# Reordered first loads, ten raw weight buffers and a pause of the background sums in a decoder layer on one core

## The chip, the core and the metric

The kernel runs on one core of one Trainium2 chip. The core has TensorE (PE in the profile, with its weight loads as PEld), VectorE (DVE), ScalarE (ACT), GpSimd (POOL) and SyncE (SP). Each takes its instructions in the order in which the compiler wrote them. Here SP and POOL also issue the DMAs. The metric is the device time of one execution in microseconds, lower is better; a kernel's time is the median of its runs.

## What is computed

One layer of a hybrid decoder for 256 tokens and a model width of 2048, all in float32. Cut to what matters here:

```python
mod = silu(c) @ w_ada + b_ada                 # 2048 -> 6 * 2048
shift1, scale1, gate1, shift2, scale2, gate2 = split(mod, 6)
h = rms_norm(x, norm1_gain) * (1 + scale1) + shift1
proj = h @ w_in                               # 2048 -> 13840 columns
qa = rms_norm(split_heads(q_sb, 6), sb_q_gain)          # stick-breaking attention, 6 heads
ka = rms_norm(split_heads(k_sb, 6), sb_k_gain)
o_sb = stick_breaking_attention(qa, ka, v_sb)
o_dil = dilated_mixture(rms_norm(q_dil), rms_norm(k_dil), v_dil)
o_gla = rms_norm(gated_linear_attention(q_gla, k_gla, v_gla, a)) * silu(r_gla)
g = sigmoid(gate_cols.reshape(256, 3, 2048))
y = g[:, 0] * (o_sb @ w_br_sb) + g[:, 1] * (o_dil @ w_br_dil) + g[:, 2] * (o_gla @ w_br_gla)
x = x + gate1 * (y @ w_out)
h = rms_norm(x, norm2_gain) * (1 + scale2) + shift2
gate, up = split(h @ w_ffn_in, 2)
x = x + gate2 * ((silu(gate) * up) @ w_ffn_out)
```

## The kernel before

**Three products for one.** Each float32 operand is split into a rounded high part and a low part (type fp32r). A product is then three matmuls: high by high, high by low and low by high (`mm3`, L180 to L182). A weight tile of two k blocks and 512 columns (128 x 1024 elements) is loaded by SP (L161) into a `raw` buffer, rounded on ScalarE into `whi` (L172), and subtracted on VectorE into `wlo` (L173). There are four buffers each of `whi` and `wlo` in the pool `wp`, and four of `raw`. `raw_tile` can add further raw buffers by name from other slots: `state["load_raws"]` for `load_weights`, `state["more_raws"]` for `load_pair`. It takes them in turn. For pairs of blocks the loads and splits have lines of their own (L228, L248, L234).

**A framework orders the work.** The kernel is written with named slots (`S("X1", ...)` takes the slot X1 when its last user is done) and priorities. The framework puts the instructions of each engine in a fixed order by priority and by its own model of time, and adds the waits. Loads, casts and splits of weights, and evictions of PSUM, stand in `prio()`, that is, 4000 places ahead of their place in the program. In `first_chunks` all of it has a still higher priority, and inside `in_order()` the program's order on PE, ScalarE and VectorE is kept.

**The start (`first_chunks`, from L632).** x comes transposed in four tiles `xT[j]` of 128 x 4 x 256, the small vectors (c, gains, biases) as `vec`, and the columns of the modulation's first chunk as `rows` from `ada_0`. `squares` (L543) squares a tile of x on ScalarE, adds its four parts in halves on VectorE (L550) and sums over partitions with a matmul by ones (L552). `root_of` (L554) makes the reciprocal root with a Newton step; between its exponential and the step it runs the work that is handed to it as `between`. The first chunk's scale and shift are made partly by PE (`on_pe`, `by_pe`, L730) and partly by VectorE (`on_dve`, L744), whose part PE sums at the end. `make_h` (L593 to L598) then writes the first chunk of the normed and modulated input h. `keep_warm(n)` (L710) issues n matmuls without use, in the numbers of `WARM`.

**The visits.** The input projection's first 13 blocks of 512 columns run while h grows chunk by chunk. `VISITS` lists which blocks run over which k; a block's partial sums lie in SBUF in between (evicted at L630, brought back at L618). `ada_chunks` meanwhile loads the columns of the modulation for the next chunk on SP's queue (L426) and reduces them on VectorE (`column_mac`, L433: one multiply-and-add with a sum per half column). In the visits `load_raws` is X1 and X2, so there are six raw buffers.

**The last visits.** `LAST` gives the k that are left of each block. Blocks 0 to 2 run, then `qk_norm` of the stick-breaking heads is called (squares on ScalarE L909, root L406 to L414, scaling on VectorE L917), then blocks 3 to 5. After that PE turns the heads (`qk_turn`, L929 and L930), and blocks 9 to 12 run with the steps of the stick-breaking attention between their products (`scores` from L949, with L952 and L953 on PE, L956 on VectorE, L959 to L961 on ScalarE). L1012 copies the product with `w_a` out of PSUM. Then come the GLA levels and blocks 6 to 8.

**Background sums.** From the last visits on, `background` makes the four other parts of the modulation (shift2, scale2, gate1, gate2), 32 half columns each, 128 in all. A step orders one 512 KB tile on GpSimd's queue (L426) into a ring of slots and runs the oldest waiting sum on VectorE (L433). At first the ring has the two slots AR0 and AR1. When a step is due is set by `tick`: a block ticks once per two k blocks with `state["rate"]`, a pair of blocks twice the rate per entry, and a step runs when the sum passes one. The rates stand in `RATE_*` and `RATES_*`. Before the output projection a loop runs steps until gate1 is there (L1469), at the third unit of the FFN `flush` runs all that is left.

**Later stages.** Two blocks for r; twelve gate blocks, of which three run singly first, six in three pairs (some entries of a pair use a fast product of seven matrices instead of eight) and three singly later, ahead of the last of the four blocks of branch products (`y_block`); then the output projection with `w_out`, the second norm, eleven FFN units, and the FFN's output.

Of the kernel before, what the change touches and what calls it, by code (L numbers as in the profile page):

```python
# [17 lines left out]
P = 128  # L18
# [14 lines left out]
SEG_SHIFT1, SEG_SCALE1, SEG_GATE1, SEG_SHIFT2, SEG_SCALE2, SEG_GATE2 = range(6)  # L33
RATE_IN, RATE_MID, RATE_GATES, RATE_PAIRS, RATE_Y, RATE_LAST = 0.7, 0.6, 0.6, (0.25, 0.2, 0.2), 0.55, 0.75

RATES_OP, RATES_FFN = (0.9, 0.7, 0.0), (0.75, 0.9, 0.7, 0.6)
LOOK = 3
DEFER = 4
AHEAD = 4000
WARM = (8, 2, 2, 2, 2, 3)  # L40
BADA = 58
RATE_FIRST = 0.7
BLOCKS_X, BLOCKS_Y, BLOCKS_Z = (1, 2, 3, 4), (5, 6, 7, 8), (9, 10, 11, 12, 0)
# [43 lines left out]
def trunk(ctx: ExitStack, tc: tile.TileContext, I, out):  # L87
# [454 lines left out]

    def squares(j, tag, a, b, sums):  # L543

        sq = S(tag, [P, 4, T]) if a == 0 else state["squares"]
        state["squares"] = sq
        nc.scalar.activation(sq[:, a:b], xT[j][:, a:b], AF.Square)
        n = (b - a) // 2
        while n:
            nc.vector.tensor_tensor(sq[:, a : a + n], sq[:, a : a + n], sq[:, a + n : a + 2 * n], op=ALU.add)  # L550
            n //= 2
        nc.tensor.matmul(sums, ones, sq[:, a, :], start=(j, a) == (0, 0), stop=(j, b) == (3, 4))  # L552

    def root_of(sums, between):  # L554


        act = nc.scalar.activation
        v, y, z, r = (x for x in S("X0", [P, 4, T]).rearrange("p a t -> a p t"))
        first = xT[0][:, 0, :]
        act(y, sums, AF.Ln, bias=eps_c[:, 0:1], scale=1.0 / D)  # L560
        nc.vector.tensor_scalar(v, sums, 1.0 / D, EPS, op0=ALU.mult, op1=ALU.add)
        act(y, y, AF.Exp, scale=-0.5)
        act(z, y, AF.Square)
        between()
        nc.vector.tensor_tensor(first, first, y, op=ALU.mult)
        nc.vector.tensor_mul(z, z, v)
        nc.vector.tensor_scalar(z, z, -0.5, 1.5, op0=ALU.mult, op1=ALU.add)
        nc.vector.tensor_tensor(first, first, z, op=ALU.mult)
        nc.vector.tensor_mul(r, y, z)
        return r  # L570
# [61 lines left out]
    def first_chunks():  # L632
# [56 lines left out]

        x_in(0, 0, 4)  # L690
        nc.sync.dma_start(vec, I["k_vec"])
        x_in(1, 0, 4)
        x_in(2, 0, 4)
        mods_in(0, 0, 4)
        x_in(3, 0, 2)
        x_in(3, 2, 4)
        mods_in(1, 0, 4)
        mods_in(2, 0, 4)
        mods_in(3, 0, 2)
        mods_in(3, 2, 4)  # L700
        load_two(0, 1, True)
# [10 lines left out]
        with in_order():  # L712
# [32 lines left out]

            squares(0, "X1", 0, 4, sums)
            keep_warm(WARM[2])
            squares(1, "X2", 0, 4, sums)
            keep_warm(WARM[3])
            squares(2, "AR0", 0, 4, sums)  # L750
            on_pe(0, 1)
            on_dve(2, 3)
            for a in (0, 2):
                squares(3, "AR1", a, a + 2, sums)
            r = state["root"] = root_of(sums, lambda: on_dve(6, 7))
            on_pe(4, 5)
            keep_warm(WARM[4])
            on_pe(8, 9)
# [12 lines left out]
            nc.vector.tensor_tensor(sh, mods[1], vec[:, o : o + 1], op=ALU.add)  # L771
            keep_warm(WARM[5])
            make_h(0, True)
# [85 lines left out]
    while steps < 4:  # L859
        next(chunks)  # L860
        steps += 1
    state["load_raws"] = ("X1", "X2")
    for n, (b, k0, k1, until) in enumerate(visits):
# [395 lines left out]
    gate2_v = columns_of("gate2")  # L1259
    bg.append(background())  # L1260
    state["rate"] = RATE_FIRST
    for b in range(0, 3):
        proj_block(*LAST[b], b)
    qk_norm(sb_parts)
    for b in range(3, 5):
# [508 lines left out]
```

## Time and profile before

| | us |
|---|---|
| median of 3 runs | 1602.7 (1599.18 to 1602.97) |
| profiled execution, device time | 1598.08 |
| its span, first to last instruction | 1596.3 |
| busy: PE, PEld | 1558.0, 1280.4 |
| busy: VectorE, ScalarE, GpSimd | 1373.4, 916.7, 71.8 |
| mean granted TensorE clock | 0.993 |
| moved by DMA | 399.20 MB, mean 250 GB/s |

The profile is of one execution. Busy time is the time in which an engine had an instruction running; matmuls overlap, and their ends are modelled, so PE counts as busy also where it isn't at its peak. The granted clock is the share of full speed that the chip gave TensorE. A row of the waits names the waiting engine, tile and line, then what released it, then the total in us, the number of times and the longest. Where an instruction waits for several things, the last one is named.

### The profile page before, as it was taken

What the parts mean: (1) busy time and instruction counts of PE and PEld (TensorE: products, weight loads), DVE (VectorE), ACT (ScalarE), POOL (GpSimd) and SP (SyncE); (2) the same over time, 40 slices, a digit from 0 to 9 for tenths busy, and PEclk for the clock granted to TensorE, in tenths of its full rate; (3) what the DMA queues carried; (4) which work ended last, traced back from release to release, by engine and by line L of the source; (5) the groups of instructions that cost most, each with busy time, mean ns of one, the idle gap of its engine ahead of it and who ended that gap; (6) DMA issues with size and microseconds to landing.
All of it is one profiled execution on the core that took longest, in us unless ns stands there. A gap on an engine that the chain in (4) does not pass through costs nothing.

```text
span 1596.3 us, 20113 instructions
## 1 busy us (share of the span) xinstructions
PE 1558.0 (98%) x7072; PEld 1280.4 (80%) x7072; DVE 1373.4 (86%) x1841; ACT 916.7 (57%) x1293; POOL 71.8 (5%) x139
## 2 busy tenths in 40 slices
PE   8999999899999999999999999999999999999998
PEld 7777777788787888888777888888888888888887
DVE  7888876879788989987988987999999999789886
ACT  6777676675755555344434745655655655455553
POOL 0000001100010000101210000000000000000000
PEclk9999999999999999999999999999999999999999
DMA  9999988766777776979989676666556566656664
GB/s 337 390 353 321 346 272 291 240 193 206 252 270 243 251 237 214 324 265 346 381 313 327 241 219 194 206 211 201 194 186 214 185 206 218 205 185 191 230 205 139
DMA packets 113924, 399.20 MB, mean 250 GB/s; under 512 B 12544, under 2 KB 13440, under 8 KB 113824
## 3 DMA queue, kind: packets, MB, share of 16 engines
q1 hardware_dynamic: 94816, 328.72, 60.6%
q0 software_dynamic: 19008, 69.21, 12.8%
q8 instruction: 55, 0.90, 0.2%
q14 instruction: 45, 0.37, 0.1%
HBM read 393.69 MB, written 4.19 MB: 249 GB/s over the span
## 4 chain that ended last, share of the span: by engine, by line
PE 50%; issue 27%; DMA 3%; POOL 3%; DVE 3%; ACT 1%; SPq 0%; POOLq 0%; DVEq 0%; ACTq 0%
PE acc L182 10%; PE acc L181 10%; PE acc L180 10%; PE misc L180 6%; PE misc L182 6%; PE misc L181 6%; DMA raw<-w_out 2%; POOL AR L426 2%; DVE wlo L173 1%; PE misc L1082 1%; POOL KC L426 1%; DMA KD<-ada_t 1%; POOL KD L426 1%; DMA AR<-ada_t 0%; DMA T<-k_lvl 0%
## 5 line engine op out<-in xcount | busy, mean ns | idle before, releaser
L181 PE MATMUL acc<-wlo,H 128*128 128x512 f32 (+1 forms) x856 | 336.3, 393 | 6.2 <-DVE wlo L173 3.9
L172 ACT CAST whi<-raw 128x1024 fp32r<-128x1024 f32 x220 | 225.9, 1034 | 200.2 <-PE acc L182 114.9
L180 PE MATMUL acc<-whi,H 128*128 128x512 f32 (+1 forms) x856 | 334.9, 395 | 5.8 <-ACT whi L172 5.8
L182 PE MATMUL acc<-whi,H 128*128 128x512 f32 (+1 forms) x856 | 335.4, 392 | 0.1
L173 DVE TENSOR_TENSOR wlo<-raw,whi 128x1024 fp32r<-128x1024 f32 x220 | 261.2, 1197 | 76.5 <-ACT whi L172 76.0
L181 PEld LDWEIGHTS acc<-wlo,H 128*128 128x128 f32 x856 | 161.9, 189 | 44.1 <-DVE wlo L173 8.8
L180 PEld LDWEIGHTS acc<-whi,H 128*128 128x128 f32 x856 | 161.6, 189 | 39.7 <-ACT whi L172 7.1
L182 PEld LDWEIGHTS acc<-whi,H 128*128 128x128 f32 x856 | 161.7, 189 | 33.5 <-DVE H L1515 0.5
L248 ACT CAST whi<-raw 128x1024 fp32r<-128x1024 f32 (+1 forms) x133 | 128.0, 977 | 75.3 <-PE acc L182 28.5
L234 DVE TENSOR_TENSOR wlo<-raw,whi 128x1024 fp32r<-128x1024 f32 (+1 forms) x133 | 147.9, 1127 | 16.4 <-ACT whi L248 15.2
L181 PE MATMUL misc<-wlo,H 128*128 128x512 f32 x285 | 111.4, 391 | 0.1
L182 PE MATMUL misc<-whi,H 128*128 128x512 f32 x285 | 110.5, 388 | 0.0
L180 PE MATMUL misc<-whi,H 128*128 128x512 f32 x285 | 108.6, 388 | 0.0
L182 PE MATMUL acc<-whi,A 128*128 128x512 f32 x221 | 86.1, 389 | 0.0
L181 PE MATMUL acc<-wlo,A 128*128 128x512 f32 x210 | 82.2, 391 | 3.6 <-DVE wlo L173 3.6
L180 PE MATMUL acc<-whi,A 128*128 128x512 f32 x210 | 82.1, 391 | 1.4 <-ACT whi L172 1.4
L173 DVE TENSOR_TENSOR wlo<-X,whi 128x1024 fp32r<-128x1024 f32 (+1 forms) x44 | 48.0, 1099 | 22.2 <-ACT whi L172 22.2
L181 PEld LDWEIGHTS misc<-wlo,H 128*128 128x128 f32 x285 | 53.5, 188 | 13.6 <-DVE wlo L173 2.9
L180 PEld LDWEIGHTS misc<-whi,H 128*128 128x128 f32 x285 | 53.5, 188 | 11.1
L182 PEld LDWEIGHTS misc<-whi,H 128*128 128x128 f32 x285 | 53.5, 188 | 10.8
L433 DVE CUSTOM_DVE_ANT_0 AR<-AR,ada,vec 128x1024 f32<-128x1024 f32 x36 | 46.0, 1278 | 13.9 <-DMA AR<-ada_t 13.9
L234 DVE TENSOR_TENSOR A<-raw,A 128x1024 fp32r<-128x1024 f32 (+2 forms) x58 | 54.3, 944 | 1.7 <-ACT A L248 0.9
(724 smaller groups left out, 3278.4 us busy)
## 6 DMA issues: line engine op xcount, KB each, us to landing
raw<-w_in SPq DMA_DIRECT2D x158, 512.0 KB, 5.1
raw<-w_ffn_in SPq DMA_DIRECT2D x137, 512.0 KB, 4.6
raw<-w_ffn_out SPq DMA_DIRECT2D x74, 512.0 KB, 4.3
AR<-ada_t POOLq DMA_DIRECT2D x70, 512.0 KB, 6.0
X<-w_in SPq DMA_DIRECT2D x39, 512.0 KB, 5.1
raw<-w_out SPq DMA_DIRECT2D x32, 512.0 KB, 7.0
OS<-ada_t SPq DMA_DIRECT2D x29, 512.0 KB, 7.3
KC<-ada_t POOLq DMA_DIRECT2D x22, 512.0 KB, 7.1
```

Of the source, the lines that this page charges most:

```text
L172: state["cast"] = nc.scalar.copy(hi[:, :n, :], raw[:, :n, :])
L173: state["split"] = nc.vector.tensor_tensor(lo[:, :n, :], raw[:, :n, :], hi[:, :n, :].bitcast(F32), op=ALU.subtract)
L180: nc.tensor.matmul(ps, lh, rh, start=start, stop=False, skip_group_check=seeded)
L181: nc.tensor.matmul(ps, lh, rl, start=False, stop=False, skip_group_check=seeded)
L182: state["mm"] = nc.tensor.matmul(ps, ll, rh, start=False, stop=stop, skip_group_check=seeded)
L234: done = nc.vector.tensor_tensor(dst, x, y, op=ALU.subtract)
L248: nc.scalar.copy(hi[:, :n, :], src)
L426: return queue.dma_start(raw, I["ada_t"][o : o + P, half * HALF : (half + 1) * HALF])
L433: return nc.vector.tensor_tensor_reduce(out=raw, in0=raw, in1=cB[:, half * HALF : (half + 1) * HALF], scale=1.0, scalar=part if half else ...
L1082: nc.tensor.matmul(ps[:n, t * N_GLA + h, :].rearrange("p (s l) -> p s l", l=L), at(f, h, t)[:, :n], odd(at(f, h, t)), start=True, stop=True,)
```

## The change

It has five parts. In the start, `vec` is loaded first, then the four tiles of x whole, then all tiles of `ada_0`; `squares` takes whole tiles with one addition on VectorE and two matmuls, and for the last tile VectorE squares one half; `root_of` has nothing in between any more, and the sums of chunks 6 and 7 follow it. The warming matmuls are dealt out anew: 23 instead of 19. In the visits `load_raws` gets four more slots, AR0, AR1, KC and KD, which makes ten raw buffers; ahead of the last visits it goes back to X1 and X2. The rate of the background is 0.0 in blocks 3 and 4, from `qk_norm` on. And eight rates have other numbers. The background's tiles stay on GpSimd's queue.

```diff
-RATE_IN, RATE_MID, RATE_GATES, RATE_PAIRS, RATE_Y, RATE_LAST = 0.7, 0.6, 0.6, (0.25, 0.2, 0.2), 0.55, 0.75
-RATES_OP, RATES_FFN = (0.9, 0.7, 0.0), (0.75, 0.9, 0.7, 0.6)
+RATE_IN, RATE_MID, RATE_GATES, RATE_PAIRS, RATE_Y, RATE_LAST = 0.8, 0.6, 0.65, (0.42, 0.25, 0.25), 0.55, 0.75
+RATES_OP, RATES_FFN = (0.9, 0.7, 0.0), (0.6, 0.75, 0.6, 0.5)
-WARM = (8, 2, 2, 2, 2, 3)
+WARM = (8, 2, 2, 2, 1, 2, 2, 4)
-RATE_FIRST = 0.7
+RATE_FIRST = 0.8
...
-    def squares(j, tag, a, b, sums):
-        sq = S(tag, [P, 4, T]) if a == 0 else state["squares"]
-        state["squares"] = sq
-        nc.scalar.activation(sq[:, a:b], xT[j][:, a:b], AF.Square)
-        n = (b - a) // 2
-        while n:
-            nc.vector.tensor_tensor(sq[:, a : a + n], sq[:, a : a + n], sq[:, a + n : a + 2 * n], op=ALU.add)
-            n //= 2
-        nc.tensor.matmul(sums, ones, sq[:, a, :], start=(j, a) == (0, 0), stop=(j, b) == (3, 4))
-    def root_of(sums, between):
+    def squares(j, tag, sums):
+        sq = S(tag, [P, 4, T])
+        if j < 3:
+            nc.scalar.activation(sq, xT[j], AF.Square)
+        else:
+            nc.scalar.activation(sq[:, :2], xT[j][:, :2], AF.Square)
+            nc.vector.tensor_tensor(sq[:, 2:], xT[j][:, 2:], xT[j][:, 2:], op=ALU.mult)
+        nc.vector.tensor_tensor(sq[:, :2], sq[:, :2], sq[:, 2:], op=ALU.add)
+        for n in range(2):
+            nc.tensor.matmul(sums, ones, sq[:, n, :], start=(j, n) == (0, 0), stop=(j, n) == (3, 1))
+    def root_of(sums):
...
-        between()
...
-        x_in(0, 0, 4)
         nc.sync.dma_start(vec, I["k_vec"])
-        x_in(1, 0, 4)
-        x_in(2, 0, 4)
-        mods_in(0, 0, 4)
-        x_in(3, 0, 2)
-        x_in(3, 2, 4)
-        mods_in(1, 0, 4)
-        mods_in(2, 0, 4)
-        mods_in(3, 0, 2)
-        mods_in(3, 2, 4)
+        for j in range(4):
+            nc.sync.dma_start(xT[j], I["x_t"][:, 4 * j : 4 * j + 4, :])
+        for j, a, b in ((0, 0, 4), (1, 0, 4), (2, 0, 4), (3, 0, 2), (3, 2, 4)):
+            nc.sync.dma_start(rows[j][:, a:b], I["ada_0"][:, 4 * j + a : 4 * j + b, :])
...
-            squares(2, "AR0", 0, 4, sums)
+            squares(2, "AR0", sums)
+            keep_warm(WARM[4])
+            squares(3, "AR1", sums)
+            on_dve(2, 3)
             on_pe(0, 1)
-            on_dve(2, 3)
-            for a in (0, 2):
-                squares(3, "AR1", a, a + 2, sums)
-            r = state["root"] = root_of(sums, lambda: on_dve(6, 7))
+            r = state["root"] = root_of(sums)
+            keep_warm(WARM[5])
             on_pe(4, 5)
-            keep_warm(WARM[4])
+            on_dve(6, 7)
+            keep_warm(WARM[6])
             on_pe(8, 9)
...
-            keep_warm(WARM[5])
+            keep_warm(WARM[7])
             make_h(0, True)
...
-    state["load_raws"] = ("X1", "X2")
+    state["load_raws"] = ("X1", "X2", "AR0", "AR1", "KC", "KD")
     for n, (b, k0, k1, until) in enumerate(visits):
...
     bg.append(background())
+    state["load_raws"] = ("X1", "X2")
     state["rate"] = RATE_FIRST
     for b in range(0, 3):
         proj_block(*LAST[b], b)
+    state["rate"] = 0.0
     qk_norm(sb_parts)
     for b in range(3, 5):
         proj_block(*LAST[b], b)
```

More of the change, by code (lines that the diff above doesn't have):

```diff
@@ L744, in on_dve @@
                         nc.vector.scalar_tensor_tensor(part, row, c, part, op0=ALU.mult, op1=ALU.add)
-            squares(0, "X1", 0, 4, sums)
+            squares(0, "X1", sums)
             keep_warm(WARM[2])
-            squares(1, "X2", 0, 4, sums)
+            squares(1, "X2", sums)
             keep_warm(WARM[3])
-            squares(2, "AR0", 0, 4, sums)
+            squares(2, "AR0", sums)
+            keep_warm(WARM[4])
+            squares(3, "AR1", sums)
+            on_dve(2, 3)
             on_pe(0, 1)
-            on_dve(2, 3)
-            for a in (0, 2):
-                squares(3, "AR1", a, a + 2, sums)
-            r = state["root"] = root_of(sums, lambda: on_dve(6, 7))
+            r = state["root"] = root_of(sums)
+            keep_warm(WARM[5])
             on_pe(4, 5)
-            keep_warm(WARM[4])
+            on_dve(6, 7)
+            keep_warm(WARM[6])
             on_pe(8, 9)
```

## The prediction

> **What bounds the kernel now.** I read the summary first, then the windows, then PE's waits, and only then the timeline around the longest of them.
>
> ```profile
> span 1596.3 us, 20113 instructions
> PE 1558.0 (98%) x7072; PEld 1280.4 (80%) x7072; DVE 1373.4 (86%) x1841; ACT 916.7 (57%) x1293; POOL 71.8 (5%) x139
> ```
>
> TensorE (PE) is busy 98% of the span. The change takes no product of the projections away, so all it can win are PE's idle stretches and those at a low clock. The windows say where these are (columns: stretch, its length, busy us and instructions of PE, PEld, DVE, ACT, POOL, granted clock, DMA share, GB/s).
>
> ```profile
> 0.00:20.00 20.00, 15.26 (x83) 12.68 (x83) 11.78 (x37) 10.10 (x16) 1.90 (x8) 0.95 0.90 330
> 40.00:60.00 20.00, 17.14 (x66) 12.61 (x65) 18.54 (x29) 13.37 (x23) 0.00 (x0) 0.91 1.03 402
> 100.00:220.00 120.00, 113.39 (x481) 88.40 (x480) 99.38 (x140) 84.38 (x130) 0.53 (x1) 1.00 0.91 324
> 274.00:326.00 52.00, 45.18 (x226) 37.49 (x224) 41.88 (x67) 34.96 (x63) 5.82 (x11) 0.93 0.71 228
> 520.00:580.00 60.00, 59.68 (x263) 49.08 (x262) 58.23 (x71) 34.19 (x38) 3.12 (x6) 1.00 0.76 251
> 580.00:600.00 20.00, 20.00 (x90) 16.53 (x90) 15.47 (x21) 9.28 (x12) 0.53 (x1) 1.00 0.67 220
> 770.00:870.00 100.00, 92.20 (x410) 73.97 (x409) 84.35 (x113) 43.12 (x52) 14.33 (x27) 1.00 0.93 349
> ```
>
> The start, the visits (to about 215 us), the stick-breaking stage (274 to 326) and the output projection (770 to 870) leave PE idle; the gate pairs (from 520) do not, but there VectorE (DVE) is full. The list of PE's own waits (total, times, longest) names what ends them:
>
> ```profile
> PE acc L180 <- ACT whi L172: 7.2, 4, 2.3
> PE misc L952 <- ACT scr L1012: 6.6, 1, 6.6
> ```
>
> The longest single one, 6.6 us at L952, is put down to ScalarE (ACT), but the timeline shows a DMA behind it (start, length, engine, line, and in brackets the idle time before and its releaser):
>
> ```profile
> 281.03 0.53 POOL L426 DMA_DIRECT2D AR<-ada_t  x1 [1.91 <-DVE mod L433]
> ...
> 286.88 1.28 DVE L433 CUSTOM_DVE_ANT_0 AR<-AR,ada,mod 128x1024 f32<-128x1024 f32 x1 [1.45 <-DMA AR<-ada_t]
> 288.09 0.43 DVE L956 TENSOR_TENSOR misc<-misc,KC 128x256 f32<-128x256 f32 x1
> ...
> 290.46 1.22 PE L952 MATMUL misc<-A,A 128*128 128x256 f32 x2 [6.57 <-ACT scr L1012]
> 293.19 0.63 PE L180 MATMUL acc<-whi,H 128*128 128x512 f32 x1
> 293.61 0.63 PE L181 MATMUL acc<-wlo,H 128*128 128x512 f32 x1
> 296.14 0.39 PE L181 MATMUL acc<-wlo,H 128*128 128x512 f32 x1
> 297.96 0.39 PE L180 MATMUL acc<-whi,H 128*128 128x512 f32 x1
> ```
>
> L433 is a background sum. Its tile was ordered at 281.03 and the sum starts at 286.88, 5.8 us later; L956, the first VectorE step of the attention scores, stands behind it in VectorE's queue, the scores' ACT steps and the copy L1012 that gives a PSUM bank back behind L956, and PE behind the bank. After the gap matmuls of 512 columns start 0.42 us apart (293.19, 293.61); from 296.14 to 297.96, eight steps on, it is 0.2275. PE is at half clock from 290.5 to about 295.
>
> **The change part by part.**
>
> *1. The pause (rate 0.0 in blocks 3 and 4, 0.8 around it).* A background step is due when ticks times rate passes a whole number; a block ticks once for each pair of k. Blocks 0, 1, 2 give 3+4+4 = 11 ticks, blocks 3 and 4 give 8, block 5 gives 3, then block 9 starts. Before: 0.7 x 23 = 16 steps by block 9's first tick, so 14 sums (two tiles are always in flight) lie ahead of L956. After: 0.8 x (11+3+1) = 12 steps, 10 sums, six of them before the pause.
>
> ```profile
> 260.79 0.69 DVE L173 TENSOR_TENSOR wlo<-X,whi 128x512 fp32r<-128x512 f32 x1
> ...
> 277.83 0.38 PE L953 MATMUL misc<-A,A 128*128 128x128 f32 x2
> ...
> L433 DVE CUSTOM_DVE_ANT_0 AR<-AR,ada,vec 128x1024 f32<-128x1024 f32 x6 | 7.7, 1280 | 7.6 <-DMA AR<-ada_t 7.6
> ```
>
> In the pause two tiles land, so sums 7 and 8 wait for nothing; they follow block 5's last split, which ended about 261.5, so tiles 9 and 10 are ordered about 263 and 264 on this clock and land 5.8 us later, by 271. L956 has its input when L953 ends, at 278.2. So I take the whole wait as gone, 6.6 us, and half of the 4.5 us at half clock, 2.3. What is late next is VectorE itself: from 274 to 326 it works 41.9 us and waits at least 7.6 for tiles (the group's row). Without the stall the stage has 52 - 8.9 = 43 us, so VectorE would be 97% full, and at rate 0.8 blocks 9 to 12 bring one sum more (9 for 8; 1.3 us). I charge 2 us of new short waits. Part 1: -6.6 - 2.3 + 2 = **-6.9**; bounds -10 (nothing returned, and sums that delay splits earlier on gone too) and -3 (two thirds returned).
>
> *2. Ten raw buffers in the visits.* 481 matmuls at 0.2275 us are 109.4 of the 120 us from 100 to 220: 10.6 us lost. PE's waits in 96 to 222, and one of the two for ACT on all engines:
>
> ```profile
> PE acc L180 <- ACT whi L172: 3.5, 2, 1.9
> PE acc L181 <- DVE wlo L173: 2.8, 5, 0.8
> ...
> 196.20 0.69 DVE L173 TENSOR_TENSOR wlo<-X,whi 128x512 fp32r<-128x512 f32 x1
> 196.91 0.33 SPq L161 DMA_DIRECT2D X<-w_in  x1
> 200.29 0.59 ACT L630 COPY A<-misc 128x512 f32<-128x512 f32 x1 [3.25 <-PE misc L182]
> 201.74 1.05 ACT L172 CAST whi<-X 128x1024 fp32r<-128x1024 f32 x1
> 202.84 0.73 PE L180 MATMUL acc<-whi,H 128*128 128x512 f32 x2 [1.91 <-ACT whi L172]
> ```
>
> The load at 196.91 could be issued only when the split at 196.20 had released buffer X; 4.8 us later ACT casts it, having stood idle 3.25 us before. With four more buffers that load goes out earlier and the cast can be placed in the idle time. The two waits cost 3.5 us, and each is followed by one of up to 0.8 for its split: some 5. The other losses are VectorE's (99.4 of 120 us), which buffers don't help. I take **-5**; bounds +1 (nothing gained, some order lost) and -9 (most of the 10.6). On SP's queue the constants for KC and KD move behind the last raw tiles in these slots; they are used from L956 on, at 288, so I cost that at nothing.
>
> The Trainium skill gives about 358 GB/s as a core's effective share of HBM (HBM Reference, Specifications); by it the visits' 324 are nearly full and this part is worth next to nothing. The 40:60 row above shows 402 GB/s; the same page says that a core streaming alone gets more, and with that the trace agrees.
>
> *3. The start.* Vectors first, x whole, one VectorE addition a tile in the squares, Newton step no longer interrupted.
>
> ```profile
> 13.78 0.47 ACT L560 ACTIVATE X<-acc,eps_c 128x256 f32<-128x256 f32 x1 [1.43 <-PE acc L552]
> 14.63 1.00 DVE L744 SCALAR_TENSOR_TENSOR T<-OS,tiny,T 128x256 f32<-128x256 f32 x2
> 17.33 1.00 DVE L744 SCALAR_TENSOR_TENSOR T<-OS,tiny,T 128x256 f32<-128x256 f32 x2
> 18.39 1.01 PE L730 MATMUL acc<-eps_c,T 128*128 128x1 f32 x4 [1.61 <-DVE T L744]
> 18.20:25.00 6.80, 6.61 (x22) 5.73 (x23) 4.55 (x9) 2.72 (x4) 0.00 (x0) 0.50 1.03 392
> ```
>
> The last x tile now comes ahead of the first modulation tile, about 1.3 us (128x1024 f32, 512 KB, at 402 GB/s) sooner; I take 0.8 of it for the row sum at 13.78. The L744 pair that filled the wait for the root (14.63) moves behind it and gives some 0.4 back. The chain to 18.39 gets 0.4 shorter. The background's first two tiles no longer load in this stage (their slots AR0 and AR1 are raw buffers now and come free late in the visits): 1 MB, 2.6 us of DMA less in front of the first weights, at DMA shares of 0.90 to 1.03; about 1.1 us of that should reach PE. Three more row-sum matmuls and four more warming ones fall into PE's idle time, 4.7 of 20 us; without that cover the four cost 0.9 (at 0.2275) to 1.7 (at 0.42). I take **-1.5**; bounds +0.5 and -4. The far end is the clock: PE runs at half from 18.2 to 25.0, which might go.
>
> The Trainium skill (TensorE: Matmul & The Clock Gate, Part 1) lets the clock fall only after an idle window of about 3.4 us. The idle time before 18.39 is 1.6 us, and the clock fell all the same; the matmuls before it have one column each. By the page's rule the shorter wait keeps the full clock, and this part would be near -3.
>
> *4. Rates later on.* Steps done by the same count, before and after: 30 and 28 at the end of the input blocks, 54 and 53 after the first gates, 64 and 67 after the gate pairs, 101 and 105 when gate1 is asked for. The pairs take 14 steps instead of 10, six of them in the first pair instead of four. At 1.28 us and a small read a sum is 1.4 us: 5.5 us more on VectorE from 520 to 640. The windows leave it 1.8 us to 580 and 4.5 to 600, so the first pair's 2.7 just fit, at the price of its lead over PE. I take **+1**; bounds 0 and +5.5 (every added sum delays a split).
>
> *5. The output projection.* It is fed by DMA: share 0.93 over 100 us, PE 7.8 us idle, and ACT waits for its weights (total, times, longest):
>
> ```profile
> ACT whi L172 <- DMA raw<-w_out: 32.7, 18, 5.1
> ```
>
> Asking for gate1 runs the steps to 107 in both kernels, in a burst of 6 before and 2 after; from there to the projection's end 13 and 12 fall due, 19 and 14 together. Five tiles fewer are 2.6 MB, 6.5 us at 402 GB/s. PE cannot gain more than its idle time, and part of that has other causes: **-3**; bounds 0 and -6. The lower FFN rates spread the last 9 steps over two units instead of one; the whole-span list names no long PE wait in the FFN lines, so 0, and at worst 1 us if a sum meets a split.
>
> **Sum.** -6.9 - 5 - 1.5 + 1 - 3 = -15.4. The profiled execution took 1598.1 us (span 1596.3 and 1.8 around it), so it would take 1582.7. The median of the timed runs, 1602.7, is 4.6 above it; the same distance gives 1587.3, as a round number **1587**.
>
> **Rivals.**
>
> *VectorE takes the wait's place.* The stick-breaking stage is 97% full without its stall, and the pairs get 5.5 us more. If part 1 leaves -3, part 4 costs 4 and the rest holds, the sum is -3 - 5 - 1.5 + 4 - 3 = -8.5: 1594. For it: 41.9 us of work in 43. Against: what is late there can run on into the next stage, where PE has blocks 6 to 8 to fill in.
>
> *The ten buffers don't do what they say.* If casts stay behind evictions in ACT's queue whatever is loaded, or DMA at 0.91 is as full as it gets, part 2 is 0 and the time 1592. For it: the eviction at 200.29 stands ahead of the cast. Against: the late load at 196.91.
>
> *Slower: weights push the columns back.* In the visits SP issues weight tiles and modulation columns in one queue. Four more weight tiles ahead are 2 MB, 5 us at 402 GB/s. If the columns' lead is less, a sum waits on VectorE as at 286.88, and PE waits for the new h. By that row 1.45 us for each of 13 chunks and 0.7 for the split behind are 28 us: -15.4 + 5 + 28 = +17.6, 1620. It decides from a lead below about 5 us. Against: PE's waits in the visits (the two rows above) don't name h, and raw loads that wait for a buffer hold the columns back today.
>
> **How the numbers follow.** Forecast as summed, 1577 to 1592: 0.50. VectorE in place, 1591 to 1598: 0.15; buffers without effect, 1588 to 1596: 0.10; both of these together or losses in other stages, 1598 to 1607: 0.14; columns late, above 1607: 0.11. A range of 1573 to 1601 leaves out the last case and two thirds of the one before: 0.2. A measurement of this kernel can tell about 0.3% (4.8 us) from no change: faster, below 1597.9, 0.75; within, 0.14; slower, 0.11.
>
> **What would show it.** Part 1: no wait of 6 us at L952, full clock there, no VectorE wait for AR just ahead of L956. Part 2: PE's two waits for ACT at L180 gone. Part 3: L560 near 13.0 us, L730's wait shorter. Part 4: more L433 in the pairs and no new PE wait there. Part 5: ACT's wait for w_out below 32.7. The prediction is wrong if VectorE waits for columns in the visits, or if PE is idle in the pairs.

## The result and the profile after

| | before | after |
|---|---|---|
| median, us | 1602.97 (1599.18 to 1605.95, 7 runs) | 1593.64 (1592.12 to 1598.23, 7 runs) |
| after / before | | 0.9947, 95% interval 0.9932 to 0.9961 |
| profiled execution, span, us | 1596.3 | 1591.1 |

The changed kernel is 0.53% faster, some 8.5 us. 15.4 us had been worked out. One run of h1_late_steps, a kernel of the experiments below, took 2616.52 us, far above its eleven others, and is left out of its median. The page of the profile after begins:

```profile
span 1591.1 us, 20160 instructions
PE 1558.7 (98%) x7082; PEld 1281.6 (81%) x7082; DVE 1373.1 (86%) x1838; ACT 917.2 (58%) x1292; POOL 71.8 (5%) x139
```

The same windows as before the change (stretch, length, busy us and instructions of PE, PEld, DVE, ACT, POOL, granted clock, DMA share, GB/s):

```profile
0.00:20.00 20.00, 17.88 (x93) 15.85 (x93) 11.40 (x34) 9.58 (x15) 0.69 (x6) 0.93 0.93 345
100.00:220.00 120.00, 113.68 (x485) 89.21 (x484) 99.58 (x140) 84.34 (x130) 1.73 (x3) 1.00 0.89 321
274.00:326.00 52.00, 48.57 (x252) 39.85 (x251) 41.61 (x68) 37.34 (x68) 5.28 (x10) 1.00 0.69 224
580.00:600.00 20.00, 16.91 (x62) 12.88 (x61) 16.08 (x23) 9.00 (x11) 1.20 (x3) 0.83 0.72 247
770.00:870.00 100.00, 98.71 (x446) 81.35 (x445) 86.03 (x111) 46.21 (x57) 13.24 (x25) 1.00 0.94 350
```

The visits (100 to 220) stand as they stood. The start, the stick-breaking stage and above all the output projection (92.20 to 98.71 us busy) are better, and 580 to 600, where PE had been full, has a hole and a lower clock. PE's waits of the whole span, the longest groups (total, times, longest):

```profile
PE acc L181 <- DVE wlo L173: 5.6, 6, 2.6
PE acc L181 <- DVE wlo L234: 4.7, 4, 2.1
PE acc L180 <- ACT whi L172: 4.3, 3, 1.9
PE misc L977 <- ACT T L972: 1.8, 1, 1.8
PE misc L948 <- ACT scr L1008: 1.6, 1, 1.6
```

(L948 was L952, L1008 was L1012; lines moved up by four.) The wait of 6.6 us is down to 1.6. But the longest wait for a split (wlo, L173) is 2.6 now and was 1.6, the waits for splits of pairs of blocks (L234) are 4.7 in all and were 2.0, and L977 is new on the list.

A table of stages makes the kernels comparable. It is read from each trace at five instructions, named by their lines before the change: PE's first L180 (the visits begin), ScalarE's first L1306 (the first gate leaves PSUM), VectorE's third L328 (the merge of the last gate pair), ScalarE's fifth L1308 (the single gates are nearly through), VectorE's first L1484 (the second norm begins). Stage 2 holds the visits and the scores, 3 the gate pairs, 5 the output projection. The column burst is the number of background steps that are not yet done when the projection asks for gate1, counted from the rates as in the prediction; they run in one burst there. The four columns at the right are PE's idle time in stages 3 and 5 (length less busy time) and the time there at a granted clock of one half.

```
stage, us                     1      2      3      4      5      6  burst   idle3  half3  idle5  half5
before                     55.8  395.1  175.0  138.7  115.4  716.3      6     2.4    3.4    7.8    0.0
e1_raws                    58.7  398.0  174.9  138.7  117.7  716.2      6     2.3    3.4    7.4    6.8
e2_start                   53.9  397.2  174.8  138.7  117.1  716.3      6     2.8    0.0    8.2    3.4
e3_pause                   59.7  396.2  175.0  138.7  123.6  716.4      8     3.1    0.0   10.5   13.7
e4_rates                   59.3  395.4  178.1  137.7  107.6  715.7      0     4.4    0.0    1.7    0.0
after                      53.9  393.5  182.1  138.7  107.1  715.9      2     6.5    6.8    1.3    0.0
f1_pause_early             57.7  396.4  174.4  138.3  116.9  716.3      1     2.1    0.0    6.1   10.2
f2_no_pause                52.6  396.7  180.1  137.9  110.3  715.7      0     4.8    3.4    2.0    3.4
f3_pairs_even              53.8  392.3  185.7  137.8  111.4  715.6      2     8.1   10.2    4.1    3.4
f4_casts_first             54.3  395.0  181.5  138.7  107.4  716.1      2     5.8    6.8    1.7    0.0
h1_late_steps              54.3  394.7  175.1  138.7  120.3  716.1      0     3.0    0.0    9.3   10.2
h2_late_steps_pause        53.8  397.9  174.6  138.9  114.0  715.9      0     2.6    0.0    5.5    3.4
h3_no_burst                58.6  396.4  175.5  138.4  110.3  716.1      1     3.0    0.0    2.4    3.4
h4_late_steps_six_raws     53.7  395.4  176.1  138.2  113.8  715.9      0     2.9    0.0    6.4    0.0
```

The first row and the row "after" give the change by stages: -1.9, -1.6, +7.1, 0, -8.3, -0.4. One execution stands behind a row, and the profiled execution of before was a quick one at its start: the five other kernels with the old start have 57.7 to 59.7 in stage 1.

The columns at the right account for stage 5. Less its idle time, and less half of its time at half clock, it is 105.6 to 107.6 us in all fourteen kernels. So the kernels differ there by PE's waits and by the clock. Of the 8.3 us that the change gains in stage 5, 6.5 are idle time; of the 7.1 that it loses in stage 3, 4.1 are idle time and 1.7 the clock.

### The profile page after: what moved, and what is told of

It is laid out like the page before. It is cut to its first block, busy times and chain, and to the rows that moved or that the text cites. A ratio compares the mean times of both kernels' runs of the same rounds, so it can differ in the third digit from the quotient of the medians.

```text
span 1591.1 us, 20160 instructions
## 1 busy us (share of the span) xinstructions
PE 1558.7 (98%) x7082; PEld 1281.6 (81%) x7082; DVE 1373.1 (86%) x1838; ACT 917.2 (58%) x1292; POOL 71.8 (5%) x139
## 4 chain that ended last, share of the span: by engine, by line
PE 54%; issue 26%; POOL 3%; DVE 2%; DMA 2%; ACT 1%; POOLq 0%; DVEq 0%; ACTq 0%
PE acc L181 11%; PE acc L182 11%; PE acc L180 11%; PE misc L180 6%; PE misc L182 6%; PE misc L181 6%; DMA AR<-ada_t 2%; POOL AR L426 1%; PE misc L1078 1%; DVE AR L433 1%; POOL KD L426 1%; DVE wlo L173 0%; POOL KC L426 0%; PE misc L1407 0%; ACT whi L172 0%
## 5 line engine op out<-in xcount | busy, mean ns | idle before, releaser
L180 PE MATMUL acc<-whi,H 128*128 128x512 f32 (+1 forms) x856 | 334.0, 393 | 5.8 <-ACT whi L172 4.3
L182 PE MATMUL acc<-whi,H 128*128 128x512 f32 (+1 forms) x856 | 334.9, 392 | 0.0
L172 ACT CAST whi<-raw 128x1024 fp32r<-128x1024 f32 x204 | 209.6, 1034 | 205.1 <-PE acc L182 139.7
L173 DVE TENSOR_TENSOR wlo<-raw,whi 128x1024 fp32r<-128x1024 f32 x204 | 241.9, 1197 | 71.9 <-ACT whi L172 71.4
L180 PEld LDWEIGHTS acc<-whi,H 128*128 128x128 f32 x856 | 161.0, 188 | 40.4 <-ACT whi L172 5.6
L182 PEld LDWEIGHTS acc<-whi,H 128*128 128x128 f32 x856 | 161.4, 189 | 33.1 <-DVE H L598 0.2
L234 DVE TENSOR_TENSOR wlo<-raw,whi 128x1024 fp32r<-128x1024 f32 (+1 forms) x133 | 147.9, 1127 | 18.4 <-ACT whi L248 17.3
L182 PE MATMUL misc<-whi,H 128*128 128x512 f32 x285 | 110.5, 388 | 0.0
L180 PE MATMUL misc<-whi,H 128*128 128x512 f32 x285 | 109.1, 389 | 1.1 <-ACT whi L172 1.1
L182 PE MATMUL acc<-whi,A 128*128 128x512 f32 x221 | 86.0, 389 | 0.0
L180 PE MATMUL acc<-whi,A 128*128 128x512 f32 x210 | 82.0, 391 | 0.0
L180 PEld LDWEIGHTS misc<-whi,H 128*128 128x128 f32 x285 | 53.4, 188 | 12.8 <-ACT whi L172 1.5
L426 POOL DMA_DIRECT2D AR<-ada_t x71 | 37.6, 530 | 560.0 <-DVE mod L433 348.6
L182 PEld LDWEIGHTS misc<-whi,H 128*128 128x128 f32 x285 | 53.5, 188 | 10.8
L234 DVE TENSOR_TENSOR A<-raw,A 128x1024 fp32r<-128x1024 f32 (+2 forms) x58 | 54.3, 944 | 3.2 <-ACT A L248 2.7
```

What stands on the lines that cost most here:

```text
L172: state["cast"] = nc.scalar.copy(hi[:, :n, :], raw[:, :n, :])
L173: state["split"] = nc.vector.tensor_tensor(lo[:, :n, :], raw[:, :n, :], hi[:, :n, :].bitcast(F32), op=ALU.subtract)
L180: nc.tensor.matmul(ps, lh, rh, start=start, stop=False, skip_group_check=seeded)
L182: state["mm"] = nc.tensor.matmul(ps, ll, rh, start=False, stop=stop, skip_group_check=seeded)
L234: done = nc.vector.tensor_tensor(dst, x, y, op=ALU.subtract)
L426: return queue.dma_start(raw, I["ada_t"][o : o + P, half * HALF : (half + 1) * HALF])
```

## The experiments

**One part at a time, on the kernel before.** First the ten raw buffers alone (e1_raws):

```diff
-    state["load_raws"] = ("X1", "X2")
+    state["load_raws"] = ("X1", "X2", "AR0", "AR1", "KC", "KD")
...
     bg.append(background())
+    state["load_raws"] = ("X1", "X2")
     state["rate"] = RATE_FIRST
```

> The kernel before with the ten raw buffers in the visits alone. Theory A (the casts stand behind the evictions in ScalarE's static order, so buffers change nothing): the two waits of PE for ScalarE at L180 stay, about 3.5 us in sum; 100 to 220 us keeps a TensorE busy time within 0.5 us of 113.4; the time is within 1.5 us of before. Rival B (the buffers help, and something else of the change took it back): the two waits fall below 1 us and the time falls by 4 to 5 us. Rival C (the buffers' worth lies at the start, because the background's first two tiles no longer load there): 0 to 40 us gains 1 to 2 us with the waits in the visits as they were.

Measured: 1602.35 us against 1601.71, ratio 1.0008 (0.9995 to 1.0021). PE's waits from 100 to 222 us in this kernel:

```profile
PE acc L180 <- ACT whi L172: 3.5, 2, 1.9
PE acc L181 <- DVE wlo L173: 2.8, 5, 0.8
```

They are those of before to the tenth. Nothing is gained at the start either (58.7), so theory A stands and B and C fall. Next, the new start alone (e2_start: the changed loads, `squares`, `root_of` and `WARM`, all else as before):

> The kernel before with the new start alone (vectors first, x whole, the new squares and root, the new warming counts). Theory A: the start's gain in the changed kernel, 1.8 us of TensorE time within 0 to 40 us, is the new order's own, so it comes here too: -1.5 to -2.5 us. Rival C (it came from the two background tiles that no longer load there): the wait before the first row products falls below 1 us but 20 to 40 us loses it again; the time is within 0.7 us of before.

Measured: 1598.76 us, ratio 0.9978 (0.9968 to 0.9987), that is -3.5 us (-5.1 to -2.1). One row of PE's waits in the first 58 us of e1_raws, which has the old start:

```profile
PE acc L730 <- DVE T L744: 1.6, 1, 1.6
```

and the same wait with the new start, in e2_start:

```profile
PE acc L724 <- DVE T L738: 0.3, 1, 0.3
```

Theory A holds, the size is above it: stage 1 is 53.8 us on average over the eight kernels with the new start and 58.3 over the six with the old. Then the pause alone (e3_pause):

```diff
-RATE_IN, ... = 0.7, ...
+RATE_IN, ... = 0.8, ...
-RATE_FIRST = 0.7
+RATE_FIRST = 0.8
...
+    state["rate"] = 0.0
     qk_norm(sb_parts)
```

> The kernel before with the pause alone (rate 0.0 in blocks 3 and 4, 0.8 before and after). Theory A: the wait of 6.6 us ahead of the scores falls to about 1.6 us and the half clock behind it goes, two waits for a split of 2 to 3 us come in its place: 240 to 300 us loses 4 to 5 us less, 300 to 420 us 2 us more, so -2 to -3.5 us in all. Rival D (the new waits at 244 and 308 us in the changed kernel come from its other parts): -6 to -9 us here.

Measured: 1607.68 us, ratio 1.0044 (1.0029 to 1.0059): slower, against both theories. PE's waits from 236 to 330 us in e3_pause:

```profile
PE misc L981 <- ACT T L976: 2.7, 1, 2.7
PE misc L952 <- ACT scr L1012: 1.2, 1, 1.2
PE acc L181 <- DVE wlo L173: 1.1, 1, 1.1
```

The scores go as theory A said: 6.6 falls to 1.2, and 2.7 and 1.1 come in its place. What neither theory had is stage 5: 123.6 us instead of 115.4. VectorE's waits from 760 to 905 us, before:

```profile
DVE AR L433 <- DMA AR<-ada_t: 4.5, 2, 3.1
DVE KD L433 <- DMA KD<-ada_t: 3.5, 3, 2.5
```

in e3_pause:

```profile
DVE KD L433 <- DMA KD<-ada_t: 5.7, 2, 3.7
DVE H L433 <- DMA H<-ada_t: 4.7, 1, 4.7
DVE KC L433 <- DMA KC<-ada_t: 3.2, 2, 2.4
```

and in the changed kernel:

```profile
DVE AR L433 <- DMA AR<-ada_t: 1.9, 2, 1.3
DVE KC L433 <- DMA KC<-ada_t: 1.1, 1, 1.1
```

In the projection sums stand at the head of VectorE's queue and wait for their tiles, with the splits of the weights behind them: by these rows 8.0 us before, 13.6 with the pause alone, 3.0 after the change. The pause puts two steps off; no later rate takes them up, and they join the burst. By the table PE idles only 2.7 us more in stage 5 than before; the larger part of the 8.2 us is the clock, at half for 13.7 us in this execution and not at all in that of before. Last, the later rates alone (e4_rates: `RATE_GATES` 0.65, `RATE_PAIRS` (0.42, 0.25, 0.25), the new `RATES_FFN`):

> The kernel before with the later rates alone (first gates, gate pairs, FFN). Theory A: the new loss at the start of the second gate pair, about 6 us of TensorE time from 580 to 600 us, comes from the sums that the higher rate puts there, and the gain of about 8 us in the output projection from the sums that no longer stand in it; both appear here and the time falls by 1 to 3 us. Rival E (the projection's gain comes from the earlier parts): the loss of 6 us alone, slower by 4 to 6 us. Rival F (the loss comes from the earlier parts, by other phases of rate and tiles): the gain alone, -7 to -9 us.

Measured: 1596.64 us, ratio 0.9977 (0.9963 to 0.9990). Stage 5 falls to 107.6, stage 3 rises to 178.1. Theory A's two effects are both there, and the time falls a little more than its 1 to 3 us. The loss in the pairs is 3.1 us here and not 6: PE idles 4.4 us in stage 3 and not 6.5, and the clock stays full, where it is at half for 6.8 us after the change.

This run also limits what the waits for tiles explain. In e4_rates VectorE's sums wait 7.3 us for tiles from 760 to 905 us (rows of 2.9, 2.3 and 2.1), almost as long as before, and yet PE idles 1.7 us in stage 5 and not 7.8. So the total of these waits does not decide; a wait costs PE only where a split that it needs next stands behind it. How much of the gain is the sums' waits, and how much their work and their bytes, was not separated.

**The burst.** The pause alone again, with `RATE_LAST` at 0.95 instead of 0.75 (f1_pause_early):

> The kernel before with the pause alone, and the rate of the last gates (RATE_LAST) at 0.95 instead of 0.75, so that one step instead of eight is left for the burst when gate1 is asked for. Theory G (what is left for that burst starves the output projection, some 2 to 3 us of TensorE time a step): TensorE's loss from 780 to 920 us falls from 22.6 us (the pause alone) to about 6, the time falls by 10 to 16 us against the pause alone, to 0.994 to 0.998 of before. Rival H (the burst doesn't matter; the pause alone was slower by its own waits in the scores): within 3 us of the pause alone, 1.003 to 1.006 of before.

Measured: 1598.35 us, ratio 0.9976 (0.9958 to 0.9994): 0.68% below the pause alone (9.3 us by the medians), by one constant. Theory G holds in the time. In the trace stage 5 falls only to 116.9, with 6.1 us idle and 10.2 at half clock, and one row makes up most of PE's waits:

```profile
PE misc L374 <- DVE T L365: 3.9, 1, 3.9
```

L374 turns a finished segment of the modulation. With the steps pushed hard against the end of the gates, sums crowd ahead of the vector step (L365) that it needs. Then the kernel before with `RATE_Y` 0.7 and `RATE_LAST` 0.8 alone (h3_no_burst), where the steps are spread over more of the way:

> The kernel before with RATE_Y 0.7 and RATE_LAST 0.8 alone: the burst falls from six steps to one. Theory G (what is left for the burst starves the projection): TensorE's loss from 780 to 920 us falls from 14 to 16 us to 6 to 9, the time by 6 to 9 us: 0.994 to 0.996 of before. Rival M (the steps cost as much where they are moved to): 0.998 to 1.001.

Measured: 1595.56 us, ratio 0.9955 (0.9940 to 0.9971), as theory G has it, with 110.3 in stage 5. PE idles 2.4 us in stage 5. **Two constants bring about as much as the whole change** (0.9955 against 0.9947, with intervals that overlap).

**The changed kernel without its pause** (f2_no_pause: the line `state["rate"] = 0.0` out, `RATE_IN` and `RATE_FIRST` at 0.7):

> The changed kernel without the pause and with the input blocks' rates at 0.7 again; everything else of it stays (start, ten buffers, later rates). By the count of steps no burst is left here (0; 2 in the changed kernel). Theory G: the projection stays at a loss of about 6 us, the wait of 5 to 6 us ahead of the scores comes back, the one at 308 us goes: slower than the changed kernel by 2 to 4 us (0.996 to 0.998 of before). Rival I (the pause is worth nothing once the burst is gone, since its wait comes back later): within 1.5 us of the changed kernel, 0.994 to 0.996.

Measured: 1592.58 us, ratio 0.9930 (0.9914 to 0.9947); with the pause it was 0.9947 (0.9932 to 0.9961). The wait is back in full:

```profile
PE misc L948 <- ACT scr L1008: 6.6, 1, 6.6
```

and yet nothing is lost. That is rival I, though 0.9930 lies just below its 0.994 to 0.996. The two kernels also differ by two steps in the burst. What the pause gave back shows in the changed kernel's timeline of VectorE ahead of the scores (start, length, engine, line; in brackets the idle time before and its releaser):

```profile
244.39 1.28 DVE L433 CUSTOM_DVE_ANT_0 AR<-AR,ada,vec 128x1024 f32<-128x1024 f32 x1 [4.93 <-DMA AR<-ada_t]
245.60 3.20 DVE L173 TENSOR_TENSOR wlo<-X,whi 128x1024 fp32r<-128x1024 f32 x2
...
282.56 1.29 DVE L433 CUSTOM_DVE_ANT_0 AR<-AR,ada,vec 128x1024 f32<-128x1024 f32 x1 [3.27 <-DMA AR<-ada_t]
...
283.77 0.43 DVE L952 TENSOR_TENSOR misc<-misc,KC 128x256 f32<-128x256 f32 x1
```

At rate 0.8 the sums ahead of the pause catch up with their tiles, one waits 4.93 us, and the split behind it is PE's new wait of 2.6. After the pause they do so again: a sum still stands right ahead of the first score step (L952 after the change). Its own wait for its tile is longer than before (3.27 us for 1.45), PE's wait behind it shorter (1.6 for 6.6). PE's idle time in the whole of stage 2 is 15.7 us before, 16.6 after the change and 17.6 without the pause. Over all traces stage 2 is 395.2 us on average with the pause (six kernels) and 396.1 without (eight); within either group it varies by 3 to 6.

**The gate pairs.** First the pair rates at 0.34, 0.3, 0.3 (f3_pairs_even):

> The changed kernel with gate pair rates 0.34, 0.3, 0.3 instead of 0.42, 0.25, 0.25: one step less in the first pair, one more after it, the same number at the end of the branch sums and the same burst of two. Theory J (the loss of 6.4 us at 587 to 592 us is the sum that waits for its tile ahead of the merge, and goes when that sum does): -4 to -6 us against the changed kernel, 0.991 to 0.993 of before. Rival K (VectorE is full in the pairs, and the loss moves to the second or third pair): within 2 us of the changed kernel.

Measured: 1597.12 us, ratio 0.9960 (0.9942 to 0.9979). Stage 3 is 185.7: the loss stays where it was, and theory J falls in this form. Rival K falls too: the loss does not move to another pair, and the time lies some 2 us by the ratios, 3.5 by the medians, above the changed kernel. VectorE at the end of the second pair, in the changed kernel:

```profile
578.03 1.27 DVE L433 CUSTOM_DVE_ANT_0 KD<-KD,ada,vec 128x1024 f32<-128x1024 f32 x1
...
579.35 1.28 DVE L433 CUSTOM_DVE_ANT_0 AR<-AR,ada,mod 128x1024 f32<-128x1024 f32 x1
...
584.56 1.28 DVE L433 CUSTOM_DVE_ANT_0 AR<-AR,ada,vec 128x1024 f32<-128x1024 f32 x1 [3.92 <-DMA AR<-ada_t]
...
585.77 0.69 DVE L328 TENSOR_TENSOR KC<-acc,T 128x512 f32<-128x512 f32 x1
...
591.10 1.21 DVE L234 TENSOR_TENSOR wlo<-X,whi 128x1024 fp32r<-128x1024 f32 x1
```

and before:

```profile
579.80 1.28 DVE L433 CUSTOM_DVE_ANT_0 KD<-KD,ada,vec 128x1024 f32<-128x1024 f32 x1
...
585.62 1.23 DVE L234 TENSOR_TENSOR wlo<-X,whi 128x1024 fp32r<-128x1024 f32 x1 [4.53 <-ACT whi L248]
586.76 0.68 DVE L328 TENSOR_TENSOR KC<-acc,T 128x512 f32<-128x512 f32 x1
```

Sums have piled up at the end of the pair, the last one waits 3.92 us for a tile, and the order behind it is another: before, the first split of the third pair (L234) stands ahead of the merge (L328), at 585.62; now it stands behind most of it, at 591.10. The wait itself is no longer than what VectorE idled there before (4.53 us, for the cast of that split). The order is the difference: ScalarE starts this cast at 584.52 before and at 584.78 after, so the split could go at 585.6 and at 585.8, and now it goes 5.3 us later than that. The weight tile of this cast also took longer, 6.7 us from the issue of its load to the cast (578.13 to 584.78) and 4.6 before (579.91 to 584.52); what that adds was not separated. e4_rates, f2_no_pause and f3_pairs_even have the new order too. So the old pair rates were put back, without the pause, and the steps that this leaves went behind the pairs (h1_late_steps: pairs 0.25, 0.2, 0.2, `RATE_Y` 0.7, `RATE_LAST` 0.8):

> The changed kernel without the pause, with the old rates in the gate pairs (0.25, 0.2, 0.2) and the steps that these leave undone put behind them (RATE_Y 0.7, RATE_LAST 0.8); no burst is left by the count. Theory J2 (the loss of 4 to 7 us at 585 to 595 us comes from a crowd of sums at the end of the second pair, the last of which waits for its tile ahead of the merge; it is the sums' place, not their number, that costs): TensorE's loss from 580 to 600 us below 1 us, the projection (780 to 920 us) at 5 to 9 us, the time 3 to 5 us below the kernel without pause that had the higher pair rates: 0.989 to 0.991 of before. Rival M (VectorE is as full behind the pairs, and the loss moves there): 0.992 to 0.995, with a new loss in 640 to 780 us.

Measured: 1599.93 us, ratio 0.9987 (0.9970 to 1.0004). Its window at the place is full again:

```profile
580.00:600.00 20.00, 20.00 (x90) 16.55 (x89) 15.97 (x22) 9.68 (x13) 0.07 (x1) 1.00 0.65 210
```

The split stands ahead of the merge again (584.03 and 585.17). So J2 is right of the pairs (stage 3 is 175.1), but the time is a miss by both theories: stage 5 is 120.3. PE's wait there and VectorE's timeline:

```profile
PE misc L374 <- DVE T L365: 4.1, 1, 4.1
```

```profile
764.80 0.17 DVE L364 CAST T<-mod 128x16 fp32r<-128x16 f32 x1
764.88 1.28 DVE L433 CUSTOM_DVE_ANT_0 AR<-AR,ada,vec 128x1024 f32<-128x1024 f32 x1
...
766.08 1.22 DVE L173 TENSOR_TENSOR wlo<-raw,whi 128x1024 fp32r<-128x1024 f32 x1
767.22 0.17 DVE L365 TENSOR_TENSOR T<-mod,T 128x16 fp32r<-128x16 f32 x1
```

A sum and a split stand between the two vector steps (L364, L365) of the turned segment, and PE waits for the second at the head of its queue. By the table PE idles 9.3 us in stage 5, 4.1 of them in this wait, and the clock is at half for 10.2 us, which costs 5.1 more. The same with the pause and `RATE_Y` 0.75 (h2_late_steps_pause):

> As h1_late_steps, but with the pause of the change (RATE_FIRST and RATE_IN 0.8, 0.0 between) and RATE_Y 0.75, so that no burst is left either. Theory I (the pause removes 9 us at the scores and gives nearly as much back in waits for sums before and after it): within 2 us of h1_late_steps. Rival N (the 4 us that the traces show between 240 and 320 us are real): 3 to 5 us faster than h1_late_steps, 0.986 to 0.988 of before.

Measured: 1593.49 us, ratio 0.9943 (0.9925 to 0.9962), 6.4 us below h1_late_steps, more than either rival allows. Stage 5 is 6.3 us shorter there, stage 2 is 3.2 longer: the difference isn't made at the scores, so it says nothing for rival N, and the pair of kernels doesn't tell the two apart. The same as h1_late_steps with six raw buffers (h4_late_steps_six_raws):

> As h1_late_steps, but with six raw buffers in the visits as before the change. Theory A (the four further buffers are worth nothing): within 1.5 us of h1_late_steps, and TensorE's loss from 40 to 220 us within 1 us of it. Rival B (they are worth something once other losses are gone): slower than h1_late_steps by 3 us or more.

Measured: 1597.63 us, ratio 0.9971 (0.9954 to 0.9988), 2.3 us below the kernel with ten, and PE's busy time from 40 to 220 us is 170.18 us against 169.98. Rival B falls; theory A's 1.5 us is passed, on the side that speaks against the buffers.

**The casts in the visits.** If ScalarE's order holds the casts up, evictions can be put behind them (f4_casts_first):

```diff
...
+        w = load_weights(w_in, k0, k1, b)
+        if waiting:
+            with tc.issue_after(state["first_cast"].ins):
+                evict(*waiting.pop())
...
```

> The changed kernel, with each visit's evictions put behind the first cast of the next visit in ScalarE's order. Theory A: the two waits for a cast at 184 and 200 us, 1.8 and 2.1 us, fall below 0.7 us each, and 3 to 4 us are gained if nothing else is held up: 0.992 to 0.993 of before. Rival L (the evictions then come late for the PSUM banks, or columns of h stand behind the casts): the waits change their place and the time stays within 1.5 us of the changed kernel. Rival B (the weights land too late, whatever the order): the waits stay, now put down to the DMA.

Measured: 1596.38 us, ratio 0.9957 (0.9942 to 0.9973), against 0.9947 of the changed kernel. PE's waits from 100 to 222 us (two lines further down in this file, so L182 is the product with whi and L183 that with wlo):

```profile
PE acc L183 <- DVE wlo L175: 6.2, 6, 1.8
PE acc L182 <- ACT whi L172: 1.7, 1, 1.7
```

and in the changed kernel:

```profile
PE acc L180 <- ACT whi L172: 3.5, 2, 1.9
PE acc L181 <- DVE wlo L173: 2.3, 4, 0.8
```

The wait for casts halves and the one for splits takes its place: 7.9 us in all instead of 5.8. So it was the order that held the casts up, and moving it gains nothing: the waits change their place, as rival L has it, and the time ends 1.6 us (by the ratios) above the changed kernel. The split of an early cast is next in line on VectorE, which is busy 99.58 of 120 us from 100 to 220 us in the changed kernel.

## Why the prediction held, and where its steps did not

1587 was predicted and 1593.64 measured, faster and inside the range of 1573 to 1601. The gain was worked out at nearly twice what came. The time lies outside the main case (1577 to 1592) and inside those of two rivals. That the sum came this close is in part luck: parts 1, 2 and 4 each promised some 5 to 6 us too much, part 5 promised 5 too little and part 3 two.

Of the prediction's own signs these came: PE's wait at L952 fell (1.6 us for 6.6) with the clock full there, L560 (now L561) starts earlier (13.29 for 13.78), L730's wait is shorter (0.5 for 1.6), and ScalarE's wait for w_out from 780 to 880 us is 10.8 for 32.7. These did not: VectorE still waits for AR just ahead of L956, PE's two waits at L180 in the visits stand, and PE is idle in the pairs, which the prediction named as a sign of being wrong.

*1. The pause: -6.9 forecast, about -1 measured in stage 2 (less than the kernels of a group differ), and two steps put off.* What was said of the wait (gone) and of the clock (1.00 from 274 to 326) came nearly so: 1.6 us are left. The step that failed is "I charge 2 us of new short waits": the stage gave back all of PE's idle time, in front of the pause as well as behind it. Nor did the prediction price the two steps that the pause leaves undone: the pause alone is 0.44% slower, and its trace has the excess in stage 5. In its cost this is the rival "VectorE takes the wait's place". But VectorE is not full there: it works 41.61 of 52 us from 274 to 326, and from 225 to 290 its sums wait 13.9 us for their tiles, where they waited 14.9 before.

*2. Ten raw buffers: -5 forecast, 0 measured.* The load did go out earlier; the step that failed is "the cast can be placed in the idle time". After the change the tile of the same cast lies in KD; SP's timeline, and how long loads into this slot took to land (smallest, median, largest):

```profile
183.56 0.38 SPq L161 DMA_DIRECT2D KD<-w_in  x1
```

```profile
DMA to landing us min/median/max: 8.1/8.5/8.9
```

ScalarE's timeline there:

```profile
195.27 1.12 ACT L618 COPY acc<-A 128x512 f32<-128x512 f32 x2
199.64 0.59 ACT L630 COPY A<-misc 128x512 f32<-128x512 f32 x1 [3.25 <-PE misc L182]
...
200.62 0.57 ACT L630 COPY A<-misc 128x512 f32<-128x512 f32 x1
201.09 1.05 ACT L172 CAST whi<-KD 128x1024 fp32r<-128x1024 f32 x1
```

The tile was there by 192.5, the eviction comes at 199.64, and the cast stands behind it all the same, with the same 3.25 us of idle time before. The order was fixed beforehand, and buffers don't change it: the second rival, to the letter. f4_casts_first, which changes the order, shortens the wait for casts.

*3. The start: -1.5 forecast, -3.5 measured* (interval -5.1 to -2.1). The new order of the start works as said, and its term was too small. The 1.1 us for the two background tiles that no longer load came to nothing: the ten buffers alone leave stage 1 at 58.7, and the new start without them has the 53.9 of the whole change. PE's idle time in stage 1 falls from 7.6 to 3.3 us; the half clock stays, 6.8 us for 6.9. Part of the difference from stage 1's -1.9 is the base: the profiled execution of before had a quick start, 55.8 us against 57.7 to 59.7 in the five others with that code.

*4. Rates in the pairs: +1 forecast, +7.1 in stage 3.* It lies above the bound of 5.5. The step that failed is "the first pair's 2.7 just fit": not the sums' own length costs, but their crowd at the end of the second pair, with the merge that the framework then puts ahead of a split, and the clock, which falls there (0.83 from 580 to 600 us). With the old rates the old order and the full window are back (h1_late_steps). Whether the order would cost as much without the sum's wait was not tried.

*5. The projection: -3 forecast, -8.3 in stage 5.* The bound of -6 was broken too. The count was right: 24 sums run in stage 5 instead of 29. The step that failed is "It is fed by DMA", by which the gain was worked out from bytes. In h3_no_burst ScalarE waits for w_out nearly as long as before (29.3 us for 32.7, from 780 to 880 us), and still PE idles 2.4 us in stage 5 and not 7.8. Of those 7.8 PE waited 4.5 for splits, which stand in VectorE's queue with the sums.

The five together, by stages of the two profiles: -1.9 (start), -1.6 (visits and scores), +7.1, -8.3 and -0.4 are -5.1; the profiled times differ by 5.2. With a usual start in place of the quick one the first term is some 3 us larger, which makes about 8, near the 8.5 of the runs.

No kernel here clearly beats the changed one. The lowest is f2_no_pause with 0.9930, and its interval (0.9914 to 0.9947) overlaps that of the changed kernel (0.9932 to 0.9961). Not tried: a larger ring in the scores and in the pairs, where the slots are taken by other tiles.

## What to carry to other kernels

Background work that waits for its own data at the head of an in-order queue can cost more by the wait and by the new order behind it than by its length; look for its place in the queue, and for what the scheduler puts behind it. A pause only moves such work: find the deadline at which it all falls due, and pay for the pause on the way there. Before a stall is priced from one execution, see whether other executions of the same code have it, and take the time at a low clock apart from the waits. Test the parts of a change one by one, since their worths don't add.

## What the runs showed of the hardware

TensorE's clock fell to half at the start though PE hardly waited. The changed kernel from 14.0 to 24.4 us:

```profile
14.00:17.40 3.40, 3.40 (x28) 3.23 (x28) 3.21 (x9) 3.37 (x8) 0.00 (x0) 1.00 1.05 394
17.40:24.40 7.00, 6.52 (x24) 5.71 (x24) 4.71 (x10) 2.72 (x4) 0.00 (x0) 0.51 0.83 311
```

PE's only wait there comes after the fall:

```profile
18.25 1.01 PE L724 MATMUL acc<-eps_c,T 128*128 128x1 f32 x4 [0.48 <-DVE T L738]
```

By the rule of the Trainium skill (TensorE: Matmul & The Clock Gate, Part 1) that the clock falls after an idle window of about 3.4 us, a shorter wait ahead of this row should have kept it up. The trace does not agree: 0.51 with a wait of 0.48 us, and PE busy for all of the 3.40 us before. Of the 28 matmuls in these, 24 have one column each; whether such matmuls count as idle was not tried.

The same waits can have the clock fall behind them or not. PE's two waits for casts in the visits are 3.5 us in all, the longest 1.9, in both the kernel before and e1_raws. The granted clock from 100 to 220 us is 1.00 in the first and 0.97 in the second, where it is at half from 191.3 to 194.7 and from 208.3 to 211.8. It fell behind these waits in seven of the 14 traces. So single traces can differ in time where their waits agree.

A background tile of 512 KB took longer to come in the pairs than at the scores. In the changed kernel it took 4.9 us in the median from order to landing (3.8 to 7.1, 12 tiles) from 270 to 330 us, and 6.2 (3.9 to 8.0, 14 tiles) from 520 to 640. The one summed at 584.56 was ordered here, in GpSimd's timeline:

```profile
577.26 0.53 POOL L426 DMA_DIRECT2D AR<-ada_t  x1 [2.95 <-DVE mod L433]
```

That is 7.3 us from order to sum, VectorE waiting; by the prediction's row at 281.03 it was 5.8.
